# Twelve of sixteen activation differences formed on GpSimd, and a weight tile on the other side of SBUF: a diffusion layer on one Trainium2 core

## The chip, the cores and the metric

The kernel runs on one core of one Trainium2 chip. The metric is device time in microseconds (us) for one execution. TensorE (PE) multiplies matrices, VectorE (DVE), ScalarE (ACT) and GpSimd (POOL) work elementwise, and SyncE (SP) issues most of the DMA transfers. Each engine runs its own instructions strictly in order and waits for others by semaphores.

## The reference

One layer over 1024 latent tokens of width 1024, with 256 context tokens. What matters here is its second half, a gated MLP with a depthwise convolution of width 3 along the tokens:

```python
h2 = rms_norm(x, norm2_g[l]) * (1.0 + sc2) + sh2
x = x + g2 * conv_ffn(h2, w_up[l], conv_w[l], conv_b[l], w_down[l])

def conv_ffn(h, w_up, conv_w, conv_b, w_down):
    u = h @ w_up                      # 1024 x 1024 by 1024 x 5632
    up = jnp.pad(u, ((0, 0), (1, 1), (0, 0)))
    u = up[:, :-2] * conv_w[0] + up[:, 1:-1] * conv_w[1] + up[:, 2:] * conv_w[2] + conv_b
    a, b = jnp.split(u, 2, axis=-1)
    return (jax.nn.silu(a) * b) @ w_down
```

Everything is float32. The first half (a modulated RMSNorm, one input projection, retention and differential attention, one output projection) comes before it and is left as it is.

## The kernel before, in words

**Products in parts.** To keep float32's accuracy on TensorE, each operand is split into a high part `hi`, rounded to the matmul format by ScalarE (`nc.scalar.copy`), and a rest `lo`, formed on VectorE as `src - hi`. A product is three passes: hi·hi, hi·lo, lo·hi (`passes`, lines 130 to 132). Splitting a weight tile is `split_op` (lines 908 and 909); splitting an activation chunk is `split_to` (955 and 956).

**Seven products instead of eight.** The up projection multiplies 2x2 blocks by a Strassen-Winograd scheme. The activations are a 2x2 block matrix B11, B12, B21, B22 (channel halves by token halves), each of four chunks of 128 channels by 512 tokens. Besides B11, B21 and B22 themselves the products need four combinations, T1 = B12 - B11, T2 = B22 - T1, T3 = B22 - B12 and T4 = B21 - T2. `turned1` forms them, after the output projection: for each chunk `c`, TensorE transposes the normalised tokens (`turned`, line 948), ScalarE brings them out of PSUM with scale and shift (line 950) into `r12` and later `r22`, and the inner helper `less` (line 1015) forms the differences in place: per chunk `r12 - b11` (T1), `r22 - r12` (T3), `r22 - b11` (T2) and `b21 - b11` (T4). That makes sixteen differences of 128x512 float32, all on VectorE, and as many splits. `turned1` is a generator: `beside(turned1(), 0.36, 0.0)` advances it by 0.36 steps after each group of three matmuls of the first products, so TensorE meets the transposes at fixed places among them.

**The weight blocks.** Block `j` of 22 takes two weight tiles, `wra` (columns of the a half) and `wrb` (of the b half), 512 KB each. `up_load(j)` allocates and loads both; their pool `wst` has two buffers of each name on the right side of SBUF. From the two tiles GpSimd forms the weight sums (`combined`, lines 1054 and 1057 to 1060): for blocks from `NSUM` = 2 on these are s1 = b1 + b2 (1057), s2 = s1 - a1 (1058), s3 = a1 - b1 (1059) and a last one in place (1060); s2 feeds the product with T2, s3 the one with T3. For blocks 0 and 1 the sums were made earlier, during the output projection. The third block (`j == NSUM`) has a place of its own for its `wrb`, in the pool `third_b`, since both `wrb` buffers are still in use then. That pool is on the right side, where raw0, the rows x1 and r12, r22 lay before it: its load waits until these have been read. Its `wra` goes to a `wst` buffer that block 0 held, so its load waits until block 0's last use of it, the split for the product with T2.

**A block's products.** `chain` is one PSUM bank that accumulates through a block: after the product with T2 ScalarE copies it to `ua` (line 1144), after the one with T3 to `ub` (1152), after the one with T4 to `ub`'s other half (1160). The next product may only go on in the bank once the copy is done. VectorE adds the other products (1147, 1153, 1159), then follows the convolution (1095 to 1097), the gate's sigmoid-weighted unit (1165) and the product of the two halves (1166).

**What sets the order.** The list of each engine's instructions is written out by a scheduler when the kernel is built; pools and the written order decide it together. On the chip nothing is reordered.

Of the kernel before, what the change touches and what calls it, by code (L numbers as in the profile page):

```python
# [12 lines left out]
ALU = mybir.AluOpType  # L13
# [15 lines left out]
NF = DFF // P  # L29
# [44 lines left out]
def kernel(  # L74
# [16 lines left out]
    nc = tc.nc  # L91
# [61 lines left out]
    with ExitStack() as p1:  # L153
# [221 lines left out]
        side = {"g": iter(()), "rate": 0.0, "due": 0.0}  # L375
# [353 lines left out]
        class Unit:  # L729
# [34 lines left out]
            def turned(self, g):  # L764
                if self.aT is None:
                    self.aT = at.tile([P, NKT, P], F32, name="aT")
                n = min(4, NKT - 4 * g)
                nc.scalar.copy(self.aT[:, 4 * g : 4 * g + n, :], self.pt[g][:, :n, :])
# [101 lines left out]
    with ExitStack() as p2:  # L870
# [5 lines left out]
        for n in range(n_units + 8):  # L876
# [6 lines left out]
            if n in (8, 10, 12, 14):  # L883
                a, i = divmod(n // 2 - 4, 2)
# [27 lines left out]
    def raw_load(name, src, pool=None):  # L912
        o = (pool or wst).tile([P, KD, P], F32, name=name)
        nc.sync.dma_start(out=o, in_=src)
        return o
# [38 lines left out]
    def split_to(src, tt, c):  # L954
        nc.scalar.copy(tt[0][:, c, :], src)
        nc.vector.tensor_tensor(out=tt[1][:, c, :], in0=src, in1=r32(tt[0][:, c, :]), op=ALU.subtract)
# [7 lines left out]
    NPRE = 3  # L964
    NSUM = 2
    def up_load(j):
        return raw_load("wra", w_up[j]), raw_load("wrb", w_up[j + NF], third_b if j == NSUM else None)

    def sums_in_place(a, b):

# [40 lines left out]
    tmpT = tmpS.enter_context(tc.tile_pool(name="tmpT", bufs=1, side="right"))  # L1011

    def turned1():
        def less(o, a, b):
            nc.vector.tensor_tensor(out=o, in0=a, in1=b, op=ALU.subtract)

        for c in range(4):
            r12 = tmpT.tile([P, 512], F32, name="r12", bufs=2)
            turned(1, c, r12, True)
            b11 = raw0[:, c, :]  # L1020
            less(b11, r12, b11)
            yield
            r22 = tmpT.tile([P, 512], F32, name="r22")
            turned(1, c + 4, r22, True)
            split_to(b11, T1, c)
            split_to(r22, B22, c)
            less(r12, r22, r12)
            less(b11, r22, b11)
            split_to(r12, T3, c)
            yield  # L1030
        for c in range(4):
            b11, b21 = raw0[:, c, :], raw0[:, c + 4, :]
            split_to(b11, T2, c)
            less(b21, b21, b11)
            split_to(b21, T4, c)
            yield
# [27 lines left out]
    ops = [combined(j) for j in range(NSUM)]  # L1064
    split_ahead = []
    beside(turned1(), 0.36, 0.0)
    for j in range(NPRE):
        chain[j] = bank("chain", psA)
# [20 lines left out]
    with ExitStack() as p4:  # L1089
# [7 lines left out]
            nc.vector.scalar_tensor_tensor(out=t[:, : L - 1], in0=u[:, 1:], scalar=w[2], in1=t[:, : L - 1], op0=ALU.mult, op1=ALU.add)  # L1097
            return t

        third_b = p4.enter_context(tc.tile_pool(name="third_b", bufs=1, side="right", reuse_waits="tile"))  # L1100
        raws.append(up_load(NSUM))
        held = {}

# [66 lines left out]
        for j in range(NF):  # L1170
            if NSUM < j + 1 < NF:
                raws.append(up_load(j + 1))
            blk = Block(j)
            blk.begin()
            if last is not None:
                last.end()
                last.gated()
            blk.middle()
            last = blk
# [31 lines left out]
    with ExitStack() as p5:  # L1211
# [19 lines left out]
        def less(o, a, b):  # L1231
            nc.vector.tensor_tensor(out=o, in0=a, in1=b, op=ALU.subtract)
# [191 lines left out]
```

## Time and profile before

| | |
|---|---|
| time, median of 3 runs | 1449.69 us (1447.68 to 1451.36) |
| span of the profiled execution | 1444.3 us |
| around the span, against the median | 5.4 us |
| PE busy in the span | 1391.0 us (96%) |
| DVE busy | 1013.2 us (70%) |
| ACT busy | 738.7 us (51%) |
| POOL busy | 336.4 us (23%) |
| stage of the change | about 797 us (first chunk) to 880 us (fourth block) |

The profiled execution's own time is not listed apart from its span; the median of the three runs is 5.4 us longer than the span, and this is taken as what lies around it (start and end of the execution). The timeline's rows read: start in us, duration in us, engine, line, operation, output<-inputs, tile form; in square brackets the idle time of the engine before the row and what ended it. Rows of a line that start closer together than their duration are pipelined.

### The profile page before, as it was taken

To read this page: it belongs to the slowest core of one execution; us is meant where nothing else is said; L and a number is where in the kernel's file an instruction comes from. 1 tells how busy PE (TensorE), PEld (TensorE's weight loads), DVE (VectorE), ACT (ScalarE), POOL (GpSimd) and SP (SyncE) were. 2 spreads that over 40 slices of the span, in tenths; PEclk is the share of its full clock that TensorE was granted. 3 is DMA by queue.
4 is the path that set the end of the run, shared out by engine and by line. 5 is a ranking of instruction groups with operands and counts; after the bars stand their busy time and mean duration, and the time that the engine had idled before them with its cause. 6 is when DMAs were issued, how large, how long until landed. Compare 5 with 4: busy or idle time off the path is not lost.

```text
span 1444.3 us, 19462 instructions
## 1 busy us (share of the span) xinstructions
PE 1391.0 (96%) x6924; PEld 1143.5 (79%) x6924; DVE 1013.2 (70%) x1509; ACT 738.7 (51%) x1409; POOL 336.4 (23%) x450
## 2 busy tenths in 40 slices
PE   7999999999899989999999999999999999999996
PEld 2587888788778779999888877888888888888885
DVE  4687454443677588889455988788777777998457
ACT  4565212232355688998414654555555545455533
POOL 0220000022688422431121043222223320000001
PEclk9999999999999999999999999999999999999999
DMA  7548754466456676680422122222222224952224
GB/s 283 218 144 292 241 190 161 161 190 189 129 160 194 161 180 157 149 150 2 187 77 85 73 89 110 110 109 99 86 90 106 109 109 166 391 208 103 102 95 175
DMA packets 107529, 217.77 MB, mean 151 GB/s; under 512 B 8932, under 2 KB 47332, under 8 KB 106536
## 3 DMA queue, kind: packets, MB, share of 16 engines
q1 hardware_dynamic: 99304, 191.62, 38.2%
q0 software_dynamic: 8128, 24.91, 7.8%
q8 instruction: 55, 0.90, 0.3%
q14 instruction: 42, 0.34, 0.1%
HBM read 159.08 MB, written 57.41 MB: 150 GB/s over the span
## 4 chain that ended last, share of the span: by engine, by line
PE 69%; DVE 8%; issue 6%; DMA 6%; POOL 3%; ACT 3%; SPq 0%; POOLq 0%; DVEq 0%; ACTq 0%
PE pv L774 5%; PE pA L742 5%; PE chain L130 5%; PE chain L132 5%; PE chain L131 5%; PE c L132 4%; PE c L131 4%; PE c L130 4%; PE pn L132 3%; PE pn L130 3%; PE pn L131 3%; PE third L132 2%; PE third L130 2%; PE third L131 2%; PE pt L762 2%
## 5 line engine op out<-in xcount | busy, mean ns | idle before, releaser
L130 PE MATMUL chain<-T,whi 128*128 128x512 f32 x264 | 103.7, 393 | 5.8 <-ACT ub L1152 3.1
L130 PE MATMUL pl<-hT,whi 128*128 128x512 f32 x256 | 107.6, 422 | 0.7 <-ACT hT L583 0.7
L131 PE MATMUL chain<-T,whi 128*128 128x512 f32 x264 | 103.5, 392 | 0.0
L132 PE MATMUL chain<-T,wlo 128*128 128x512 f32 x264 | 103.1, 391 | 0.0
L131 PE MATMUL pl<-hT,whi 128*128 128x512 f32 x256 | 101.6, 397 | 1.6 <-DVE sm L115 1.3
L132 PE MATMUL pl<-hT,wlo 128*128 128x512 f32 x256 | 100.9, 394 | 0.0
L745 DVE TENSOR_REDUCE mt<-pA 128x1 f32<-128x1280 f32 x64 | 95.3, 1490 | 3.3 <-PE pA L742 1.2
L742 PE MATMUL pA<-ks,qhl 128*128 128x512 f32 (+1 forms) x384 | 91.4, 374 | 5.0 <-ACT p L749 5.0
L132 PE MATMUL c<-whi,ghl 128*128 128x512 f32 x232 | 90.4, 390 | 0.2 <-DVE ghl L1228 0.2
L130 PE MATMUL c<-whi,ghl 128*128 128x512 f32 x232 | 90.3, 389 | 0.0
L131 PE MATMUL c<-wlo,ghl 128*128 128x512 f32 x232 | 90.2, 389 | 0.0
L749 ACT ACTIVATE p<-pA,mt 128x1280 f32<-128x1280 f32 x64 | 85.5, 1336 | 4.6 <-DVE mt L745 4.5
L116 POOL TENSOR_TENSOR sm<-sm,mhalf 128x1 f32<-128x1 f32 x26 | 16.7, 641 | 294.9 <-DVE sm L115 294.8
L1057 POOL TENSOR_TENSOR cmb<-wrb 128x512 f32<-128x512 f32 x20 | 26.8, 1341 | 250.1 <-DMA wrb<-w_up 135.9
L908 ACT CAST whi<-cmb 128x512 fp32r<-128x512 f32 x62 | 38.6, 623 | 87.1 <-PE chain L131 65.3
L742 PEld LDWEIGHTS pA<-ks,qhl 128*128 128x128 f32 x384 | 68.8, 192 | 17.6 <-ACT p L749 6.1
L130 PE MATMUL pn<-whi,hT 128*128 128x512 f32 x192 | 77.8, 405 | 0.0
L774 PE MATMUL pv<-va,aT 128*128 128x128 f32 x640 | 77.0, 275 | 0.1
L399 ACT ACTIVATE st<-pn 128x512 f32<-128x512 f32 x30 | 17.9, 598 | 114.7 <-PE pn L132 97.2
L908 ACT CAST whi<-wra 128x512 fp32r<-128x512 f32 x55 | 33.7, 622 | 82.9 <-PE third L131 42.3
L132 PE MATMUL pn<-whi,hT 128*128 128x512 f32 x192 | 75.5, 393 | 0.0
L131 PE MATMUL pn<-wlo,hT 128*128 128x512 f32 x192 | 75.1, 391 | 0.0
(320 smaller groups left out, 4006.2 us busy)
## 6 DMA issues: line engine op xcount, KB each, us to landing
wm<-w_mod SPq DMA_DIRECT2D x32, 512.0 KB, 4.4
raw<-w_in SPq DMA_DIRECT2D x28, 512.0 KB, 4.5
wra<-w_up SPq DMA_DIRECT2D x24, 512.0 KB, 3.2
wrb<-w_up SPq DMA_DIRECT2D x23, 512.0 KB, 3.5
W<-w_down SPq DMA_DIRECT2D x44, 256.0 KB, 6.0
ad<-s SPq DMA_DIRECT2D x20, 512.0 KB, 3.7
wra<-ad SPq DMA_DIRECT2D x20, 512.0 KB, 3.2
wrb<-ad SPq DMA_DIRECT2D x18, 512.0 KB, 4.1
```

What stands on the lines that cost most here:

```text
L116: nc.gpsimd.tensor_tensor(out=out_ap, in0=out_ap, in1=mhalf[:, :n], op=ALU.pow)
L130: mm(ps, lh, rh, start=first, stop=False, skip_group_check=more)
L131: mm(ps, lh, rl, start=False, stop=False, skip_group_check=more)
L132: mm(ps, ll, rh, start=False, stop=last, skip_group_check=more)
L399: nc.scalar.activation(st.rearrange("p h e -> p (h e)"), pt, func, scale=scale)
L742: mm(self.pa[m][:, c0:c1], self.q[:, i, m, qs], self.k[:, m, c0:c1], start=(i == 0), stop=(i == 1))
L745: nc.vector.tensor_reduce(out=self.mt[:, m : m + 1], in_=self.pa[m][:, :LK], axis=AX.X, op=ALU.min)
L749: nc.scalar.activation(self.p[m], self.pa[m][:, :LK], AF.Exp, scale=-1.0, bias=self.mt[:, m : m + 1], accum_out=self.s[:, m : m + 1])
L762: nc.tensor.transpose(self.pt[g][:, i, :], self.p[0][:, (4 * g + i) * P : (4 * g + i + 1) * P], ident)
L774: mm(self.pv, self.aT[:, c, :], self.v[:, c, :], start=(c == 0), stop=(c == NKT - 1))
L908: nc.scalar.copy(hi, src)
L1057: nc.gpsimd.tensor_tensor(out=s1, in0=b1, in1=b2, op=ALU.add)
```

## The change

Two things are changed. In `turned1` the helper `less` takes an engine; the first difference of each chunk (T1) stays on VectorE, and the three others of each chunk, twelve of the sixteen, go to GpSimd. The pool `third_b` moves from the right side of SBUF to the left (where it follows the buffers of the combinations, on ground that the output projection's weights held), and for the third block `up_load` issues the load of `wrb` ahead of that of `wra`.

```diff
     def up_load(j):
-        return raw_load("wra", w_up[j]), raw_load("wrb", w_up[j + NF], third_b if j == NSUM else None)
+        if j == NSUM:
+            b = raw_load("wrb", w_up[j + NF], third_b)
+            return raw_load("wra", w_up[j]), b
+        return raw_load("wra", w_up[j]), raw_load("wrb", w_up[j + NF])
...
     def turned1():
-        def less(o, a, b):
-            nc.vector.tensor_tensor(out=o, in0=a, in1=b, op=ALU.subtract)
+        def less(o, a, b, eng=nc.gpsimd):
+            eng.tensor_tensor(out=o, in0=a, in1=b, op=ALU.subtract)
 
         for c in range(4):
             r12 = tmpT.tile([P, 512], F32, name="r12", bufs=2)
             turned(1, c, r12, True)
             b11 = raw0[:, c, :]
-            less(b11, r12, b11)
+            less(b11, r12, b11, nc.vector)
             yield
...
-        third_b = p4.enter_context(tc.tile_pool(name="third_b", bufs=1, side="right", reuse_waits="tile"))
+        third_b = p4.enter_context(tc.tile_pool(name="third_b", bufs=1, reuse_waits="tile"))
```

The lines behind the edit stand three lower in the changed kernel (`less` is 1018 there, s1 1060, s2 1061, the copy to `ua` 1147). The first place is VectorE's list, from the first difference to the split of block 0's weights for T2 (`wlo_8013`); here are its first eleven rows before (r12_7740 and r22_7758 belong to the first chunk, r12_7794 to the second; yT11 is the low part of T1 or B22).

```order
L1015 TENSOR_TENSOR raw0_7039<-r12_7740,raw0_7039 128x512
L1015 TENSOR_TENSOR r12_7740<-r22_7758,r12_7740 128x512
L956 TENSOR_TENSOR yT11_4752<-r22_7758,yT01_4750 128x512
L956 TENSOR_TENSOR yT11_4752<-raw0_7039,yT01_4750 128x512
L956 TENSOR_TENSOR T31_7720<-r12_7740,T30_7719 128x512
L1015 TENSOR_TENSOR raw0_7039<-r22_7758,raw0_7039 128x512
L1015 TENSOR_TENSOR raw0_7039<-r12_7794,raw0_7039 128x512
L909 TENSOR_TENSOR wlo_7848<-wra_7422,whi_7847 128x512
L1015 TENSOR_TENSOR r12_7794<-r22_7811,r12_7794 128x512
L956 TENSOR_TENSOR yT11_4752<-raw0_7039,yT01_4750 128x512
L956 TENSOR_TENSOR yT11_4752<-r22_7811,yT01_4750 128x512
```

The same place on VectorE in the changed kernel:

```order
L1018 TENSOR_TENSOR raw0_7039<-r12_7740,raw0_7039 128x512
L956 TENSOR_TENSOR yT11_4752<-r22_7758,yT01_4750 128x512
L956 TENSOR_TENSOR yT11_4752<-raw0_7039,yT01_4750 128x512
L956 TENSOR_TENSOR T31_7720<-r12_7740,T30_7719 128x512
L1018 TENSOR_TENSOR raw0_7039<-r12_7794,raw0_7039 128x512
L909 TENSOR_TENSOR wlo_7848<-wra_7422,whi_7847 128x512
L956 TENSOR_TENSOR yT11_4752<-raw0_7039,yT01_4750 128x512
L956 TENSOR_TENSOR yT11_4752<-r22_7811,yT01_4750 128x512
```

From the first L1015 to `wlo_8013` the list has 39 rows before and 28 now: the twelve differences are gone, and one split of T4 that stood behind `wlo_8013` stands ahead of it. All these rows but one (an addition out of PSUM) read both inputs from SBUF. The second place is GpSimd's list behind the last sum of block 1 (`cmb_7728`), in the changed kernel; wrb_8007 and wra_8009 are the third block's tiles.

```order
L1057 TENSOR_TENSOR cmb_7728<-wrb_7428,wra_7426 128x512 [waits PE_49,Activation_49]
L1018 TENSOR_TENSOR r12_7740<-r22_7758,r12_7740 128x512 [waits DMAHW4_49,DMAHW5_49,DMAHW3_49,DMAHW6_49,DVE_49,Activation_49]
L1018 TENSOR_TENSOR raw0_7039<-r22_7758,raw0_7039 128x512 [waits DVE_49]
L1018 TENSOR_TENSOR raw0_7039<-raw0_7039 128x512 [waits Pool_49]
...
L1018 TENSOR_TENSOR r12_7886<-r22_7904,r12_7886 128x512 [waits DVE_49,Activation_49]
L1018 TENSOR_TENSOR raw0_7039<-r22_7904,raw0_7039 128x512 [waits DVE_49]
L1018 TENSOR_TENSOR raw0_7039<-raw0_7039 128x512 [waits Pool_49]
L1060 TENSOR_TENSOR cmb_8120<-wrb_8007 128x512 [waits DMAHW3_49]
L1061 TENSOR_TENSOR cmb_8121<-cmb_8120,wra_8009 128x512 [waits DMAHW4_49,DVE_49,Pool_49]
```

Before, the third block's s1 followed `cmb_7728` directly; now the twelve differences stand between them. The third place is ScalarE's list around block 0's copy to `ua` (chain_7730 is block 0's bank, cmb_8121 the third block's s2), before:

```order
L908 CAST whi_8131<-wrb_7428 128x512 [waits PE_49]
L1144 COPY ua_7787<-chain_7730 128x512 [waits PE_49]
L1095 ACTIVATE tconv_8067<-ua_7787,cl_63 128x1024 [waits DVE_49,Activation_49]
L908 CAST whi_8167<-cmb_8121 128x512 [waits Pool_49]
L1152 COPY ub_8011<-chain_7730 128x512 [waits PE_49]
```

and in the changed kernel:

```order
L908 CAST whi_8131<-wrb_7428 128x512 [waits PE_49]
L908 CAST whi_8167<-cmb_8121 128x512 [waits PE_49,Pool_49]
L1147 COPY ua_7787<-chain_7730 128x512 [waits PE_49]
L1098 ACTIVATE tconv_8067<-ua_7787,cl_63 128x1024 [waits DVE_49]
L908 CAST whi_8185<-cmb_8120 128x512 [waits PE_49,Activation_49]
L1155 COPY ub_8011<-chain_7730 128x512 [waits PE_49]
```

The rounding of the third block's s2, which waits for GpSimd, stood behind the copy to `ua` and ahead of the copy to `ub`; now it stands ahead of both. SyncE's list still has the two loads as its next weight loads, with wrb first, and the load of wra still waits for VectorE's `wlo_8013`.

## The prediction

> **What bounds the kernel now.** I read the page first, then the windows around the change, the waits of TensorE, and the timeline of each engine there.
>
> ```profile
> span 1444.3 us, 19462 instructions
> PE 1391.0 (96%) x6924; PEld 1143.5 (79%) x6924; DVE 1013.2 (70%) x1509; ACT 738.7 (51%) x1409; POOL 336.4 (23%) x450
> ```
>
> TensorE is busy 96% of the span, so only its gaps can be won, and whatever makes a new gap is lost. By stages (columns: stretch, its length, then busy time of PE, PEld, DVE, ACT, POOL):
>
> ```profile
> 799.08:822.83 23.75, 23.75 (x117) 19.55 (x117) 23.64 (x41) 20.15 (x36) 0.00 (x0) 1.00 0.00 1
> 1000.00:1100.00 100.00, 100.00 (x443) 82.81 (x442) 80.45 (x92) 52.86 (x76) 27.49 (x20) 1.00 0.30 110
> ```
>
> The first stretch is the one of the differences: TensorE never idle, VectorE as full (23.64 of 23.75), GpSimd empty. The second is the steady run of later blocks: TensorE has no gap at all, a matmul each 100/443 = 0.226 us. A delay that reaches the steady run is not caught up there. TensorE's waits at the first blocks:
>
> ```profile
> PE chain L130 <- ACT ub L1152: 3.1, 1, 3.1
> PE chain L130 <- ACT ua L1144: 2.7, 2, 2.1
> ```
>
> Where the 3.1 comes from, in order of time:
>
> ```profile
> 799.08 0.69 DVE L1015 TENSOR_TENSOR raw<-r,raw 128x512 f32<-128x512 f32 x1
> 822.15 0.68 DVE L909 TENSOR_TENSOR wlo<-wra,whi 128x512 fp32r<-128x512 f32 x1
> 822.99 0.33 SPq L914 DMA_DIRECT2D wra<-w_up  x1
> 823.50 0.33 SPq L914 DMA_DIRECT2D wrb<-w_up  x1
> 825.55 0.59 ACT L1144 COPY ua<-chain 128x512 f32<-128x512 f32 x1 [2.35 <-PE chain L132]
> 828.71 1.29 POOL L1057 TENSOR_TENSOR cmb<-wrb 128x512 f32<-128x512 f32 x1 [32.35 <-DMA wrb<-w_up]
> 830.08 2.12 POOL L1058 TENSOR_TENSOR cmb<-cmb,wra 128x512 f32<-128x512 f32 x1
> 832.24 0.62 ACT L908 CAST whi<-cmb 128x512 fp32r<-128x512 f32 x1 [3.12 <-POOL cmb L1058]
> 832.76 0.58 ACT L1152 COPY ub<-chain 128x512 f32<-128x512 f32 x1
> 833.39 0.67 PE L130 MATMUL chain<-T,whi 128*128 128x512 f32 x1 [3.05 <-ACT ub L1152]
> ```
>
> VectorE ends its list with the split of block 0's weights at 822.83, only then is the third block's `wra` buffer free, its loads go out at 822.99 and 823.50, GpSimd's s2 ends at 832.20, and ScalarE, which stands at the rounding of s2, does the copy to `ub` late. So VectorE's list sets the date of the loads, and the loads that of the copy.
>
> **VectorE's list.** The change takes twelve rows out of it, each about 0.69 us long:
>
> ```profile
> L1015 DVE TENSOR_TENSOR raw<-r,raw x8: 681/682/686, 799.1 to 814.3; 128x512 f32<-128x512 f32 x8
> L1015 DVE TENSOR_TENSOR r<-r,r x4: 683/684/692, 799.9 to 812.5; 128x512 f32<-128x512 f32 x4
> ```
>
> They overlap a little: 39 rows in 23.75 us are 0.61 a row. The 28 rows that are left would take 17.1 us. But GpSimd now works beside them, on the same kind of operands, and this the trace has priced at the fourth block:
>
> ```profile
> 860.57 1.53 POOL L1057 TENSOR_TENSOR cmb<-wrb 128x512 f32<-128x512 f32 x1 [6.12 <-DVE wlo L909]
> 861.47 1.18 DVE L909 TENSOR_TENSOR wlo<-cmb,whi 128x512 fp32r<-128x512 f32 x1
> 862.17 1.62 POOL L1058 TENSOR_TENSOR cmb<-cmb,wra 128x512 f32<-128x512 f32 x1
> 862.57 1.77 DVE L909 TENSOR_TENSOR wlo<-wra,whi 128x512 fp32r<-128x512 f32 x1
> 863.75 1.74 POOL L1059 TENSOR_TENSOR cmb<-wra,wrb 128x512 f32<-128x512 f32 x1
> 864.87 1.17 DVE L909 TENSOR_TENSOR wlo<-wra,whi 128x512 fp32r<-128x512 f32 x1
> 865.57 1.63 POOL L1060 TENSOR_TENSOR wrb<-wra,cmb 128x512 f32<-128x512 f32 x1
> ```
>
> Read the ends: POOL 862.10, DVE 862.65, POOL 863.79, DVE 864.34, POOL 865.49, DVE 866.04, POOL 867.20. They take turns, one GpSimd and one VectorE row each 1.70 us (862.10, 863.79, 865.49, 867.20), and nothing runs at once. A GpSimd row therefore costs VectorE 1.70 - 0.61 = 1.09 us while VectorE always has work. Twelve cost 13.1. The list ends at 799.08 + 17.1 + 13.1 = 829.3, not at 822.83: **6.5 us later**, though it is twelve rows shorter. Bounds for the price of a GpSimd row: 0, as where VectorE idles or reads PSUM, and 1.29, its whole length alone (the row at 828.71). I take 1.09, since the rows are of the same size, type and engines. The price at which the list ends as before is (23.75 - 17.1)/12 = 0.55.
>
> [...]
>
> ```profile
> 822.61 0.39 PE L130 MATMUL chain<-T,whi 128*128 128x512 f32 x1
> ```
>
> TensorE meets the same delay earlier. Between its need of T1's last chunk and block 0's product with T2 (822.61) stand 39 matmuls, 8.8 us, so it asks at 813.8. The chunk's split is the 20th VectorE row, with some seven GpSimd rows ahead: 799.08 + 20 x 0.61 + 7 x 1.09 = 819, a wait of five us, and the product with T2 at about 828. This isn't added: the list's end is later. ScalarE's eviction of `r22` now waits for GpSimd too, with the casts of T1 to T4 queued behind it; that is in the turns.
>
> **The third block's loads.** `wrb` no longer waits for raw0's ground and is in long before; its part costs nothing, and s1 is done while `wra` is awaited. But `wra` still waits for the split at the list's end: 829.3 + 0.16 (822.83 to 822.99) = 829.5.
>
> ```profile
> DMA to landing us min/median/max: 3.1/3.2/11.2
> ```
>
> That is the `wra` tile's loads; I take 3.2, as it now travels ahead of the rest (5.2, from 823.50 to 828.71, is the other end, where the pair shared the queue). Landed at 832.7, s2 until 834.0 (1.29), its rounding until 834.6 (0.62). And here the new order bites: the copy to `ua` stands behind this rounding, so it starts at 834.6 instead of 825.55, 9.0 later.
>
> **From the copy to the steady run.** Before, 13.8 us lay between the copy at 825.55 and the matmul at 839.36, since the copy to `ub` was late. That wait falls away. What is left is a chain of rows:
>
> ```profile
> 829.15 1.93 DVE L1096 SCALAR_TENSOR_TENSOR tconv<-ua,cl,tconv 128x1023 f32<-128x1023 f32 x1 [1.37 <-ACT tconv L1095]
> 840.68 1.28 DVE L1096 SCALAR_TENSOR_TENSOR tconv<-ub,cl,tconv 128x1023 f32<-128x1023 f32 x1
> 835.95 1.28 ACT L1165 ACT_TABLE_LOAD   x1 [2.08 <-DVE tconv L1097]
> 837.24 1.06 ACT L1165 ACTIVATE tconv<-tconv 128x1024 f32<-128x1024 f32 x1
> 838.73 0.59 ACT L1144 COPY ua<-chain 128x512 f32<-128x512 f32 x1
> 839.36 0.50 PE L130 MATMUL chain<-T,whi 128*128 128x512 f32 x1 [0.67 <-ACT ua L1144]
> ```
>
> Copy to L1096: 829.15 - 825.55 = 3.6; L1096 itself 1.9, as s3 runs beside it again; the addition to `ub` 0.6; L1097 1.3; table load 1.3; activation to the matmul 839.36 - 837.24 = 2.1. Sum 10.8. TensorE stands at block 1's product with T3 at 834.6 + 10.8 = 845.4 instead of 839.36: **6.0 us later**. Between, it has 31 matmuls (7.0 us) from about 835.3, so it is done at 842.3 and waits 3.1. What such a wait costs more shows here (two rows behind the 3.05 us wait, and two at the 2.07 us one):
>
> ```profile
> 833.86 0.63 PE L131 MATMUL chain<-T,whi 128*128 128x512 f32 x1
> 834.28 0.63 PE L132 MATMUL chain<-T,wlo 128*128 128x512 f32 x1
> 871.70 0.50 PE L130 MATMUL chain<-T,whi 128*128 128x512 f32 x1 [2.07 <-ACT ua L1144]
> 872.03 0.40 PE L131 MATMUL chain<-T,whi 128*128 128x512 f32 x1
> ```
>
> After 3.05 us matmuls last 0.63, after 2.07 they are at 0.40 at once. Before paid this stretch too, ahead of 839.36; in the changed kernel it would fall behind it. A slow matmul takes 834.28 - 833.86 = 0.42 from start to start and not 0.226, so a stretch of eight costs 1.6. I count it, since 3.1 is on the side of 3.05; the other end is 0. The 2.07 us wait at 871.70 I leave as it is (its end would be -2.1).
>
> **Sum.** +6.0 + 1.6 = +7.6 us: the profiled execution would go from 1444.3 to 1451.9, and with the 5.4 us around it from the median of 1449.69 to **1457.3**. A measurement of this kernel tells about 0.3% (4.4 us) from no change.
>
> **Rivals.** *The rows run side by side (0.14).* Then VectorE's list isn't the limit. The last eviction of `r22`:
>
> ```profile
> 811.51 0.78 ACT L950 ACTIVATE r<-pt,m 128x512 f32<-128x512 f32 x1
> ```
>
> GpSimd's last three differences follow it with 1.37 each (828.71 to 830.08), until 816.4, casts and splits until 818, `wra` is in at 822, and the copy to `ua` runs at its old 825.55. With 10.8 from there TensorE is at 836.4, 3.0 earlier: 1446.7, and 1444.6 where the 2.07 us wait goes too. It decides below 0.55 us per GpSimd row. For it: GpSimd is empty there and the twelve rows fit its time; against it: the seven rows above.
>
> *The delay is mostly given back (0.14).* The turns come as reckoned, but the 3.1 us wait stays under what slows the clock, and the 2.07 us wait is gone, as the third block's weights then lead: 6.0 - 2.1 = +3.9, 1453.6. For it: 2.07 us cost no clock. Against it: the 2.07 wait came from VectorE's own rows, which stay.
>
> *It runs away (0.12).* Full 1.29 per row (+2.4), a load of 5.2 (+2.0): +12.0, 1461.7. [...]
>
> *The change doesn't do what it says* in one half in any case: `wrb` goes first, but `wra` and s2, which ScalarE waits for, come no sooner.
>
> **How the numbers follow.** Forecast 0.60, 1454 to 1461. The range leaves out most of the first rival and the far end of the third: 1449.5 to 1462. Faster by over 0.3%: half of the first rival, 0.07. Within 0.3%: its other half and most of the second, 0.20. Slower: the rest, 0.73.
>
> **What would show it.** Right: GpSimd's twelve rows at 1.6 to 1.7 us instead of 1.3, VectorE's rows beside them at 1.2 to 1.8, taking turns; `wlo` of block 0 ending near 829; the load of `wra` behind it; TensorE waiting some five us for T1's last chunk and again for the copies to `ua`. Wrong: GpSimd's rows at 1.3 with VectorE's at 0.69 beside them, the copy to `ua` still at 825 to 826, or the first product of the fifth block, before at
>
> ```profile
> 874.55 0.39 PE L130 MATMUL chain<-yT,whi 128*128 128x512 f32 x1
> ```
>
> not later by 4 us or more.

## The result and the profile after

The changed kernel takes 1458.53 us (median of 4 runs, 1456.91 to 1460.3) beside 1450.34 us for the kernel before (4 runs, 1447.68 to 1451.36). The ratio of the medians is 1.0056; the ratio estimated from all runs is 1.0066, with a 95% interval of 1.0047 to 1.0086: slower, by 0.5 to 0.9%. The forecast was 1457.3 us. The page of the profiled execution after:

```profile
span 1455.7 us, 19463 instructions
PE 1398.5 (96%) x6924; PEld 1147.9 (79%) x6924; DVE 1018.9 (70%) x1497; ACT 740.3 (51%) x1409; POOL 352.6 (24%) x462
```

Twelve instructions have gone from VectorE (1509 to 1497), yet its busy time has grown from 1013.2 to 1018.9 us. That is the result in one line: what was taken away came back as waiting that the profile counts as work (VectorE's rows of 0.68 us take up to 1.78 beside GpSimd's). This run's time was 1457.44, so 1.7 us lie around the span, not the 5.4 that the front matter inferred from a span of one run and a median of others.

In this execution the stage begins 1.38 us later than before (first difference at 800.46, not 799.08), from small waits hundreds of microseconds ahead of the change. Differences below are given with these 1.38 us taken off. The stage by windows (stretch, length, then busy time of PE, PEld, DVE, ACT, POOL, each with its rows), from the first difference to the end of block 0's split, and in the steady run:

```profile
800.46:830.16 29.70, 23.81 (x101) 18.38 (x101) 29.12 (x30) 19.67 (x34) 19.27 (x12) 0.89 0.05 18
1000.00:1100.00 100.00, 100.00 (x443) 82.81 (x442) 78.22 (x90) 50.96 (x74) 29.26 (x22) 1.00 0.31 111
```

The stretch was 23.75 us and is 29.70. VectorE is still full in it (29.12), and TensorE, which never paused there before, is busy for 23.81 of it. The steady run is the same as before: nothing is given back. Grouped by line and shape, GpSimd's differences and three of VectorE's groups in the stage (busy us, then mean ns of one):

```profile
L1018 POOL TENSOR_TENSOR raw<-r,raw 128x512 f32<-128x512 f32 x4 | 6.7, 1680 | 2.5 <-DVE yT L956 2.5
L1018 POOL TENSOR_TENSOR raw<-raw 128x512 f32<-128x512 f32 x4 | 6.4, 1611 | 0.3
L1018 POOL TENSOR_TENSOR r<-r,r 128x512 f32<-128x512 f32 x4 | 6.2, 1547 | 6.8 <-ACT r L950 6.1 <-DVE raw L1018 0.7
L956 DVE TENSOR_TENSOR T<-r,T 128x512 fp32r<-128x512 f32 x4 | 6.0, 1490 | 0.0
L1018 DVE TENSOR_TENSOR raw<-r,raw 128x512 f32<-128x512 f32 x4 | 4.9, 1228 | 0.0
L1047 DVE TENSOR_TENSOR ua<-second,ua 128x512 f32<-128x512 f32 x1 | 0.7, 678 | 0.0
```

VectorE rows that took 0.68 us before now average 1.2 to 1.5 in the groups shown (one that waits for its turn is counted as busy); the one that reads an input from PSUM (`ua<-second`) keeps its 0.68, beside GpSimd's row of 813.57. TensorE's waits in the stage and the blocks after it, and the rows that answer to those of the chain before, in order of time:

```profile
PE fifth L130 <- ACT yT L955: 4.5, 1, 4.5
PE chain L130 <- ACT ua L1147: 4.1, 2, 2.1
...
```

```profile
820.99 0.55 PE L130 MATMUL fifth<-yT,whi 128*128 128x512 f32 x1 [4.47 <-ACT yT L955]
827.21 0.33 SPq L914 DMA_DIRECT2D wrb<-w_up  x1
827.42 0.63 PE L131 MATMUL fifth<-yT,whi 128*128 128x512 f32 x1
829.48 0.68 DVE L909 TENSOR_TENSOR wlo<-wra,whi 128x512 fp32r<-128x512 f32 x1
830.18 0.33 SPq L914 DMA_DIRECT2D wra<-w_up  x1
833.43 1.39 POOL L1061 TENSOR_TENSOR cmb<-cmb,wra 128x512 f32<-128x512 f32 x1 [1.52 <-DMA wra<-w_up]
833.70 0.39 PE L130 MATMUL chain<-T,whi 128*128 128x512 f32 x1
836.45 0.62 ACT L908 CAST whi<-cmb 128x512 fp32r<-128x512 f32 x1 [2.15 <-PE chain L131]
836.97 0.58 ACT L1147 COPY ua<-chain 128x512 f32<-128x512 f32 x1
847.59 0.50 PE L130 MATMUL chain<-T,whi 128*128 128x512 f32 x1 [2.05 <-ACT ua L1147]
885.78 0.56 PE L130 MATMUL chain<-yT,whi 128*128 128x512 f32 x1
```

TensorE waits 4.47 us for T1's last chunk and then runs at 0.63 us a matmul for a while (the granted clock is 0.53 from 820.99 to 828.21, and 1.00 from there to 833.70, with matmuls of 0.40), so its product with T2 begins at 833.70 and not 822.61. VectorE's list ends late, and the load of `wra` goes out behind it. The copy to `ua` stands at 836.97 and not 825.55, the product with T3 at 847.59 and not 839.36, the fifth block at 885.78 and not 874.55. From there to the end of the span it is 569.9 us, before 569.75.

### The profile page after: what moved, and what is told of

Its sections match the earlier page's. It is cut to its first block, busy times and chain, and to the rows that moved or that the text cites. A ratio compares the mean times of both kernels' runs of the same rounds, so it can differ in the third digit from the quotient of the medians.

```text
span 1455.7 us, 19463 instructions
## 1 busy us (share of the span) xinstructions
PE 1398.5 (96%) x6924; PEld 1147.9 (79%) x6924; DVE 1018.9 (70%) x1497; ACT 740.3 (51%) x1409; POOL 352.6 (24%) x462
## 4 chain that ended last, share of the span: by engine, by line
PE 71%; DVE 9%; DMA 5%; issue 3%; ACT 3%; POOL 3%; SPq 0%; POOLq 0%; DVEq 0%; ACTq 0%
PE chain L130 5%; PE chain L131 5%; PE chain L132 5%; PE pv L774 5%; PE pA L742 5%; PE c L132 4%; PE c L131 4%; PE c L130 4%; PE pn L131 3%; PE pn L132 3%; PE pn L130 3%; PE third L132 2%; PE third L131 2%; PE third L130 2%; PE pt L762 2%
```

## The experiments

The theory that was tested: GpSimd's rows and VectorE's rows with both inputs in SBUF don't run at once but in turns. Rival A: the cost is GpSimd's own slowness, and the splits that wait for it. Rival B: the cost is the other half of the change, the place and order of the third block's weights. To keep noise ahead of the stage out, the table gives for each kernel's profiled execution the stretch from the first difference to the end of the last split of T4, and the time from that first difference to the end of the span; the ratio is the one estimated from all runs.

| kernel | stretch, us | from there on, us | ratio to before (95%) |
|---|---|---|---|
| before | 24.36 | 645.2 | |
| after | 29.09 | 655.2 | 1.0066 (1.0047 to 1.0086) |
| differences only | 29.08 | 654.3 | 1.0055 (1.0035 to 1.0075) |
| weights' side only | 24.37 | 646.0 | 0.9998 (0.9985 to 1.0011) |
| idle rows that read | 33.90 | 657.3 | 1.0062 (1.0040 to 1.0084) |
| idle rows that write | 24.36 | 648.5 | 1.0018 (1.0005 to 1.0032) |
| T4's four only | 25.93 | 649.1 | 1.0043 (1.0030 to 1.0056) |
| after, early half | 29.08 | 653.7 | 1.0056 (1.0040 to 1.0072) |
| before, early half | 24.37 | 649.7 | 1.0045 (1.0029 to 1.0060) |
| idle rows, one column | 24.36 | 644.7 | 1.0024 (1.0008 to 1.0039) |

The middle column is one execution of each kernel. Two executions of one kernel (before, early half) agree in it to 0.1 us, but the first difference starts anywhere from 797.5 to 803.5 us in these profiles, so the medians differ from this column by up to 5 us.

**The differences only.** The edit of `turned1` on the kernel before, and nothing else:

```diff
-        def less(o, a, b):
-            nc.vector.tensor_tensor(out=o, in0=a, in1=b, op=ALU.subtract)
+        def less(o, a, b, eng=nc.gpsimd):
+            eng.tensor_tensor(out=o, in0=a, in1=b, op=ALU.subtract)
...
-            less(b11, r12, b11)
+            less(b11, r12, b11, nc.vector)
```

> The kernel before with only the twelve differences on GpSimd; the third block's second weight tile stays on its old side and is loaded after the first one. Theory (each GpSimd difference beside a full VectorE makes the pair take turns: VectorE's own row of 0.68 us becomes about 1.75, so twelve moved rows save 12 x 0.68 = 8.2 us and cost about 12 x 1.08 = 13 us): VectorE's list of the stage ends 5 to 7 us later than before, the kernel is 6 to 10 us slower, so all of the change's cost is here. Rival A (GpSimd's own slowness: a difference takes 1.6 us instead of 0.68 and the splits wait for it): the same time, but VectorE's other rows stay at 0.68 us and VectorE shows idle time instead, some 6 us of it. Rival B (the place and the order of the third block's weights make the change slow): within 2 us of before.

Measured: 1456.21 us beside 1447.31, and a stretch of 29.08 us, the changed kernel's to 0.01. The rows beside each other have the same durations as after, VectorE's idle time in the stretch is 0.6 us, not 6. So the cost sits in this half, which puts rival B out, and not in VectorE waiting for results, which puts rival A out.

**The weights' side only.** The kernel after with `eng=nc.vector` as the default of `less`.

> The kernel after with the twelve differences put back on VectorE; only the third block's second tile is on the other side and loaded first. Theory: VectorE's rows of the stage all take 0.68 us, its list ends where it did before (within 0.5 us), and the time is that of before, within 0.3% (1446 to 1452 us); at best 1.5 us less if the second tile lands earlier. Rival A says the same. Rival B: 1456 us or more.

Measured: 1448.1 us beside 1447.31, no difference. Here a row showed that nobody had expected. The third block's s1 starts at 822.59, beside a full VectorE:

```profile
822.59 8.74 POOL L1060 TENSOR_TENSOR cmb<-wrb 128x512 f32<-128x512 f32 x1 [22.50 <-DMA wrb<-w_up]
829.49 0.69 DVE L909 TENSOR_TENSOR wlo<-wrb,whi 128x512 fp32r<-128x512 f32 x1
830.09 0.69 DVE L1150 TENSOR_TENSOR ua<-fifth,ua 128x512 f32<-128x512 f32 x1
```

It lasts 8.74 us instead of 1.29, while VectorE's rows keep their 0.69: it did not get a turn until VectorE came to a row that reads PSUM (830.09; 831.33 less 1.29 is 830.04). In these rows the two engines excluded each other, but not by turns. What decides that became the second question.

**Idle rows that read, idle rows that write.** The kernel before, and behind the last difference of each chunk three GpSimd rows that nobody needs; in the second kernel they only write, behind a difference of one column that holds them in their place:

```diff
+        idle = tmpT.tile([P, 512], BF16, name="idle")
...
+            for _ in range(3):
+                nc.gpsimd.tensor_tensor(out=idle, in0=b11, in1=b11, op=ALU.subtract)
```

```diff
+            nc.gpsimd.tensor_tensor(out=idle[:, :1], in0=b11[:, :1], in1=b11[:, :1], op=ALU.subtract)
+            for _ in range(3):
+                nc.gpsimd.memset(idle, 0.0)
```

> The kernel before, with all differences on VectorE, and twelve more GpSimd rows of 128x512 that read a chunk of the turned activations (both inputs, a finished one), three behind each chunk, and write a spare bf16 tile that nobody reads. No instruction waits for them but the three sums of the third block behind them on GpSimd, and the load of that block's second tile. Theory: nothing is saved, and twelve pairs take turns at about 1.7 us each, so VectorE rows beside them show 1.7 us, VectorE's list of the stage ends 12 x 1.08 = 13 us later than before, and the kernel is 9 to 15 us slower. Rival A (GpSimd's rows hurt only those who wait for their results): VectorE's rows stay at 0.68 us, within 2 us of before. Rival B: also within 2 us of before.

> As the run with twelve idle GpSimd rows, but each of the twelve rows only writes the spare tile (a memset of 128x512 bf16), behind one difference of 128x1 for each chunk that puts them at the same place in the list. Theory: it is the reading of SBUF that takes turns, so VectorE's rows stay near 0.68 us and the time is that of before within 2 us. If the writes take turns too, VectorE shows rows of 1 us and more beside the memsets and the time is 3 us or more above before; then the theory's word 'reading' is too narrow.

Measured: the reading rows cost 9.9 us (1457.22 beside 1447.31) though no VectorE row waits for them; this too speaks against rival A. The third group of them, and the rows beside them:

```profile
815.40 4.25 POOL L1031 TENSOR_TENSOR idle<-raw 128x512 bf16<-128x512 f32 x3 [2.50 <-DVE raw L1015]
815.78 1.52 DVE L956 TENSOR_TENSOR T<-r,T 128x512 fp32r<-128x512 f32 x1
817.22 1.52 DVE L1015 TENSOR_TENSOR r<-r,r 128x512 f32<-128x512 f32 x1
818.67 1.52 DVE L956 TENSOR_TENSOR yT<-raw,yT 128x512 fp32r<-128x512 f32 x1
820.12 0.68 DVE L956 TENSOR_TENSOR yT<-r,yT 128x512 fp32r<-128x512 f32 x1
```

Three turns, then 0.68 again. A turn is 1.45 us here and not 1.70 (these rows have one source tile and a bf16 result; which of the two shortens the turn was not tried), so a row costs VectorE 0.85 (1.45 less its pitch of 0.60); eleven full turns, and 0.24 for the one that began beside a PSUM row, give 9.6, and the stretch is 9.54 longer. The expectation took 1.08 and was 3.5 too high. The writes cost the stretch nothing: twelve memsets of 0.53 us, no VectorE row of the stage longer than before. So twelve rows that read lengthened the stretch by 9.54 us, and twelve that only write by none. What the second one loses (2.5 us) comes of its rows of one column. One of them was shut out:

```profile
813.71 14.97 POOL L1030 TENSOR_TENSOR idle<-raw 128x1 bf16<-128x1 f32 x1 [1.35 <-DVE raw L1015]
```

It reads raw0 until 828.7, and the load of the third block's `wrb`, on that ground, is issued 29.5 us behind the first difference instead of 24.4; TensorE then waits 5.5 us for the copy to `ub`, before 3.1.

**T4's four only.** `less(b21, b21, b11, nc.gpsimd)` on the kernel before, the other twelve on VectorE.

> The kernel before with only the four differences of T4 on GpSimd, the last ones of the stage. Theory (a price for each pair of turns): the stretch from the first difference to the last split of T4, 24.36 us before and 29.08 with twelve, is 24.36 + 4/12 x 4.72 = 25.9 us; no early wait of TensorE (T1 and T3 are formed as before), so the time is 1 to 3 us above before. Rival (the cost is that of the chain through the two row buffers of T3's difference, which make TensorE wait 4.5 us for T1): nothing of it is left with T4 alone, the stretch is within 0.5 us of 24.36 and the time within 1 us of before.

Measured: a stretch of 25.93, as forecast to 0.03, but by other means, and 1452.77 us beside 1446.85, 5.9 more and not 1 to 3.

```profile
803.96 1.68 POOL L1015 TENSOR_TENSOR raw<-raw 128x512 f32<-128x512 f32 x1 [6.68 <-DVE raw L1015]
808.67 1.68 POOL L1015 TENSOR_TENSOR raw<-raw 128x512 f32<-128x512 f32 x1 [3.04 <-DVE raw L1015]
814.59 9.55 POOL L1015 TENSOR_TENSOR raw<-raw 128x512 f32<-128x512 f32 x2 [4.24 <-DVE raw L1015]
816.32 0.74 PE L130 MATMUL fifth<-yT,whi 128*128 128x512 f32 x2 [1.60 <-ACT yT L955]
823.58 2.34 DVE L956 TENSOR_TENSOR T<-raw,T 128x512 fp32r<-128x512 f32 x3 [1.85 <-ACT T L955]
```

Two differences took their turn, the third was shut out until VectorE ran out of work at 821.7, and then VectorE waited 1.85 us for T4. So here the shut-out difference lengthened the stretch by coming late, and a price for each pair does not tell it all. That this wait cost the kernel time is not shown: the expectation "no early wait of TensorE" failed. T1's last chunk was late all the same. TensorE waited 1.60 us for it and ran slow behind it (rows of 0.63 us from 819.02 to 820.30, ahead of the wait 0.39), so that its product with T2 began 27.46 us behind the first difference, before 23.53. Those 3.9 us are all that this execution loses from the first difference on.

**After, early half.** The prediction let the load of `wra` and s2 set the copy to `ua`; the rounding ahead of that copy shows a wait for TensorE. To tell them apart, the half of `wra` that s2 and s3 read gets a tile of its own:

```diff
+    def halves(src):
+        a1 = third_b.tile([P, 4, P], F32, name="a1")
+        nc.sync.dma_start(out=a1, in_=src[:, 0:4, :])
+        a2 = wst.tile([P, KD, P], F32, name="wra")
+        nc.sync.dma_start(out=a2[:, 4:8, :], in_=src[:, 4:8, :])
+        return a1, a2[:, 4:8, :]
...
-            return raw_load("wra", w_up[j]), b
+            return halves(w_up[j]), b
...
```

> The kernel after, with the half of the third block's first weight tile that its sums two and three read in a tile of its own, which does not wait for the last split of the first block's weights. The prediction held that this load (issued at the end of VectorE's list, landed 3.2 us later) sets the first copy of the stage's results; the trace of after says that TensorE's product with T2 came last there. If TensorE is it: the copy to the first block's upper half stands where it did (within 0.7 us of 36.5 us behind the stage's first difference), and the time is within 2 us of after (1456.5 to 1460.5 beside a before of 1450.3, or ratio 1.0045 to 1.008). If the load is it: the copy comes 2 to 3 us earlier and the time is 2 to 4 us less.

Measured: the load leaves 2.5 us earlier against the stage's start, the rounding still waits for TensorE, and the copy comes 35.59 us behind the first difference, after 36.51, before 26.47. The ratio is 1.0056, that of after within both intervals.

```profile
833.05 0.39 PE L130 MATMUL chain<-T,whi 128*128 128x512 f32 x1
835.80 0.62 ACT L908 CAST whi<-cmb 128x512 fp32r<-128x512 f32 x1 [2.15 <-PE chain L131]
836.32 0.58 ACT L1155 COPY ua<-chain 128x512 f32<-128x512 f32 x1
```

TensorE came last, here as in the kernel after. The copy's 0.9 us are not the load's: the product with T2 itself began 32.32 us behind the first difference, after 33.24, since the slow matmuls behind the wait for T1 ended sooner (10 rows of 0.62 us and more, after 13). That is more than the 0.7 us that the expectation allowed for, but the trace shows no gain to the copy from the earlier load.

The same holds for the other kernels with differences on GpSimd. Counted from the first difference, the product with T2 began later than before by 9.7 us (after), 9.0 (differences only), 8.8 (this one) and 3.9 (T4's four), and the time from the first difference on is longer by 10.0, 9.1, 8.5 and 3.9. So in these four the cost equals, within 0.4 us, what TensorE loses ahead of its product with T2: the waits for T1 and the slow matmuls behind them. That is the balance and not every step: behind the copy the kernel after wins 3.2 us back, as the wait of 3.1 us is gone, and loses 3.0 again in two more slow stretches. With the idle rows that read it doesn't hold (8.9 and 12.1).

**Before, early half.** The same tile in the kernel before, with `third_b` opened ahead of the pool `up`, on ground that is free after the last transposes. It was meant to beat both kernels, by ending the wait of 3.1 us.

> The kernel before, all differences on VectorE, with the same half in a tile of its own, and both that tile and the second weight tile on ground that is free as soon as TensorE has done its last transposes (they are laid out ahead of the pool of the convolution's tiles). In the kernel before, the sum two of the third block runs at 830.08 to 832.20, ScalarE's rounding of it waits 3.12 us and TensorE 3.1 us for the copy behind that rounding. Theory: the loads are issued 6 to 8 us earlier, sum one runs beside the full VectorE (one pair of turns, 0.4 to 1.1 us on VectorE's list, or none if it is shut out as in the run with the weights' side alone), sum two when VectorE has split the first combination (about 827), so the rounding comes some 3 us earlier, the wait of 3.1 us falls to under 1, and the time is 2 to 4 us below before. Rival (turns): the sums push VectorE's list back by 3 us and more, and the time is that of before or up to 3 us above.

Measured: 1454.05 us beside 1446.85, slower; a second profile shows the same rows. s1 was shut out until VectorE's list had ended (824.9):

```profile
812.89 13.15 POOL L1068 TENSOR_TENSOR cmb<-wrb 128x512 f32<-128x512 f32 x1 [18.06 <-DMA wrb<-w_up]
827.41 0.62 ACT L908 CAST whi<-cmb 128x512 fp32r<-128x512 f32 x1 [5.76 <-POOL cmb L1069]
827.93 0.58 ACT L1155 COPY ua<-chain 128x512 f32<-128x512 f32 x1
```

The rounding of s2 is 3.3 us earlier against the stage's start, as expected, but the scheduler put it ahead of the copy to `ua`, as in the kernel after, and the copy is 3.9 later: TensorE waits 7.8 us for two copies, before 5.8 in three waits. The theory missed the order of ScalarE's list, which is fixed when the kernel is built.

> The kernel before with the early half once more, for a second profile: the first was of its fastest run (1449.09 us; the median was 1454.05), and showed the third block's sum one shut out for 13.15 us and TensorE waiting 7.8 us for two copies behind ScalarE's rounding of sum two. If the slow runs come from turns, sum one takes 1.3 to 1.8 us here and VectorE shows a row of 1.8; if shutting out is the rule, the same 13 us row shows at a time of 1452 us or more, and the difference to 1449 lies in the granted clock.

Both profiles have the row of 13.15 us and 649.7 and 649.8 us from the first difference on; the 6 us between them lie ahead of the stage.

**Turn or shut out?** Four kernels were for this. The first is the one with idle rows, one column wide:

> The run with twelve idle GpSimd rows that read, but each row reads and writes one column (128x1) instead of 512. In the run with memsets two of four such narrow rows lasted 1.72 and 14.97 us beside a full VectorE whose rows stayed at 0.68 us, and the wide rows took turns. If the width decides: these rows are shut out until VectorE pauses or reads PSUM, several of them show 2 us and more, VectorE's rows stay at 0.68 to 0.75 us and the stretch of the stage within 0.5 us of 24.36. If the row's width only sets the price of a turn: the rows take 0.3 to 0.8 us each, VectorE's rows beside them about 0.2 us more, and the stretch is 1 to 3 us longer. The time is within 3 us of before in both.

Measured: neither. All twelve rows came in at the next row of VectorE (1.72 us for three), and VectorE's rows stayed at 0.68. The times scatter from 1444.14 to 1454.54 us and the profile is of the fastest execution, so what makes the ratio 1.0024 is not shown. The other three compute nothing of the reference: runs of VectorE rows, with a GpSimd difference released by one of them. In short, for independent rows (`zt_before` is the result of the trial before, which ties each trial to it):

```python
for r in range(16):
    nc.vector.tensor_tensor(out=outs[r % 4], in0=zt_before if r == 0 else s0, in1=xt if r == 3 else s1, op=sub)
    if r == 3:
        nc.gpsimd.memset(xt[:, :fill], 0.0)
        nc.gpsimd.tensor_tensor(out=zt, in0=xt, in1=s1, op=sub)
```

> A kernel that computes nothing of the reference: 36 trials, in each VectorE runs 16 rows of 128x512 with two inputs in SBUF, and a GpSimd difference is released by the fourth row, after a memset of 16 to 456 columns that shifts its start against VectorE's rows in steps. Trials 1 to 12: the GpSimd row is 128x512 and VectorE's rows do not depend on each other; 13 to 24: each VectorE row reads what the one before wrote; 25 to 36: as the first twelve with a GpSimd row of one column. In the traces so far some GpSimd rows came in at VectorE's next row boundary (VectorE row 1.5 to 1.8 us) and some were shut out until VectorE stopped (8.7 to 15 us). If the moment of the start against VectorE's rows decides: within a group of twelve the trials divide by the memset's length, one stretch of lengths turned and another shut out. If the dependence of VectorE's rows decides: the first and second group differ as a whole. If the width decides: the third group differs as a whole. If it is chance: no order in it. Where every trial takes turns, shutting out needs something that this kernel lacks.

Measured: neither the start's phase nor the width decided here. With independent rows the trials alternated strictly, turn, shut out, turn, at 512 columns (1.27 to 1.81 us against 7.73 to 8.06) and at one (0.20 to 0.74 against 6.66 to 6.99); with rows that each read the one before, all twelve took turns (1.26 to 1.60 us; each of those VectorE rows starts 0.03 us behind the end of the one before it). GpSimd's timeline:

```profile
7.00 1.47 POOL L116 TENSOR_TENSOR z<-x,s 128x512 f32<-128x512 f32 x1
17.74 8.06 POOL L116 TENSOR_TENSOR z<-x,s 128x512 f32<-128x512 f32 x1
28.65 1.40 POOL L116 TENSOR_TENSOR z<-x,s 128x512 f32<-128x512 f32 x1
```

> Five groups of ten trials of the kind of the last run (16 VectorE rows each, one GpSimd difference of 128x512 released by the fourth row; nothing of the reference is computed). There the trials with independent VectorE rows took turns and were shut out one after the other, whatever the start's phase, and those whose rows each read the row before all took turns. Two things alternated there: the tile that GpSimd reads, and whether VectorE had paused since GpSimd's row before (it pauses behind a shut-out row, not behind one that took its turn). Group 1 changes the tile every second trial only: if the tile decides, the trials go turn, turn, shut, shut; if the pause decides, turn, shut, turn, shut. Group 2 makes VectorE pause behind each trial: if the pause decides, all take turns. Group 3: each VectorE row reads the row before the last; if it is the reading of the row just ahead that lets GpSimd in, this group behaves as independent rows. Group 4: two GpSimd rows in a trial: if the pause decides, the second of a pair is shut out. Group 5 repeats the chained rows: all turns.

Measured: with the tile changed every second trial still turn, shut, turn, shut (1.38 and 7.94 us; VectorE pauses 1.15 us behind a shut-out one); with a pause behind each trial ten turns of ten (1.32 to 1.38); rows that read the row before the last gave turn and shut in alternation, as independent ones (1.38 and 8.00); chained rows took turns (1.50). So in these trials the pause decided, not the tile; the chained rows, with a pause of 0.03 us at each, fit that. Two differences in a trial both took turns (3.04 us for the pair) or both were late (9.34): that part was expected otherwise, and fits if a turn itself counts as a break.

> Trials of 22 independent VectorE rows, each trial behind a pause of VectorE (nothing of the reference is computed). Group 1, 14 trials: the GpSimd difference of 128x512 is released by the row k behind the pause, k from 1 to 14. Group 2, 12 trials: a first difference is released by row 2 and takes its turn, a second one by row 2+k, k from 2 to 13. Group 3: as group 2, with a GpSimd memset of 512 columns behind the first difference. So far every difference that asked up to 6 VectorE rows behind a pause or a turn took its turn, with one exception behind a memset, and those that asked 7 rows and more behind one were shut out. Theory (a stretch of some 7 unbroken VectorE rows, 4.2 us, shuts GpSimd out): group 1 turns up to k of about 6 and is shut out above; group 2 alike, counted from the first turn. Rival (each stretch of VectorE's rows gives GpSimd one turn, whenever it asks, and is then closed): group 1 takes turns at every k, the second difference of group 2 is shut out at every k. If the memset matters, group 3 differs from group 2.

Measured: a clear edge, and the rival is out. Behind a turn the edge is near the 4.2 us of the theory, behind a pause it comes sooner than the expected six rows. Here VectorE's first row and GpSimd's difference in the fourth and the fifth trial of the first group, and the first and second difference in the trials k = 7 and k = 8 of the second:

```profile
51.61 0.69 DVE L111 TENSOR_TENSOR o<-z,s 128x512 f32<-128x512 f32 x1 [1.44 <-POOL z L116]
54.85 1.58 POOL L113 TENSOR_TENSOR x<-s,s 128x512 f32<-128x512 f32 x1 [3.28 <-DVE o L111]
67.45 0.69 DVE L111 TENSOR_TENSOR o<-z,s 128x512 f32<-128x512 f32 x1 [1.44 <-POOL z L116]
71.30 10.61 POOL L113 TENSOR_TENSOR x<-s,s 128x512 f32<-128x512 f32 x1 [3.88 <-DVE o L111]
311.08 1.57 POOL L113 TENSOR_TENSOR x<-s,s 128x512 f32<-128x512 f32 x1 [2.08 <-DVE o L111]
316.36 1.58 POOL L113 TENSOR_TENSOR x<-s,s 128x512 f32<-128x512 f32 x1 [3.70 <-DVE o L111]
327.98 1.58 POOL L113 TENSOR_TENSOR x<-s,s 128x512 f32<-128x512 f32 x1 [2.07 <-DVE o L111]
333.86 7.60 POOL L113 TENSOR_TENSOR x<-s,s 128x512 f32<-128x512 f32 x1 [4.30 <-DVE o L111]
```

Behind a pause of VectorE, a request after 3.24 us (51.61 to 54.85) took its turn, one after 3.85 (67.45 to 71.30) and all later ones were shut out until VectorE stopped (10.61 down to 5.19 us). Behind a turn, 3.71 (312.65 to 316.36) still turned, 4.30 (329.56 to 333.86) did not. With a memset in between it was the same: 3.70 turned (1.57 us), 4.31 did not (7.60). The layer's kernels fit: in the kernel with T4's four, 3.03 us behind the last turn came in and 4.24 was shut out, though VectorE had ended a row out of PSUM 2.5 us before; after's longest gaps, 2.56 and (s1) 3.97, came in; the 8.74 and 13.15 us rows asked more than ten microseconds behind VectorE's last pause. One thing stays open: the idle rows of one column didn't delay VectorE (its rows kept 0.68 to 0.69), and three of them came in at 810.16, 11.7 us behind VectorE's last pause, where the wide rows' edge would have shut them out.

## Why the prediction was right

- **The turns.** Forecast: VectorE's list ends 6.5 us later, at 1.09 us for each GpSimd row. Measured: 23.75 to 29.70, 5.95 later. 28 rows at 0.61 and 0.59 of idle time leave 12.0 us for twelve rows, 1.0 each: the first (801.28) began while VectorE waited, one (813.57) ran beside a PSUM row. The idle rows, whose results nobody needs, show that it is the sharing. Right, and for the reason given; that all twelve took turns was luck of the list, since GpSimd never let more than 2.56 us pass between them. One reading behind the price is wrong, "nothing runs at once": at the fourth block VectorE's rows of 860.87 (0.67 us) and 864.26 (0.68), which read PSUM and are not among the seven shown, ran beside GpSimd's. The turns that end at 863.79 and 867.20 have no such row in them, so the 1.70 us stand.
- **The full price.** 1.29, a GpSimd row's whole length alone, was the upper bound and the third rival's +2.4. No run shows a row that cost VectorE that much: the rows say 1.0 on average, 1.09 for a full turn. Which engine waited differed: after's VectorE rows took up to 1.78 us in turns, and a shut-out GpSimd row 13.15.
- **The loads.** `wra` was forecast to leave at 829.5 and to land 3.2 later; it left at 830.18 (828.80 with the 1.38 off), and s2 began 3.25 later. Wrong: "`wrb` no longer waits for raw0's ground and is in long before". It left at 827.21, as the split of T3's last chunk ended, which reads r12 (in the kernel with the weights' side only it left right behind that split too). So its new ground is, by all appearance, in part that of r12, and the account of that ground ahead of the prediction is incomplete; addresses were not read. It cost nothing, as s2 had to await `wra` anyway.
- **The copy to `ua`.** Forecast 9.0 later, measured 10.0. The size was nearly right, the reason was not: the step "This isn't added: the list's end is later" failed. TensorE's own delay was put at a product with T2 "at about 828"; it began at 833.70 (832.3 with the 1.38 off), as the wait for T1 ended at 820.99 and slow matmuls (0.63) filled the next 7 us. Of the 9.7 us, 4.47 are the wait for T1, put at five; 1.4 are two short waits (0.77 for an eviction by ScalarE, 0.61 for T1's low part); most of the rest are the slow matmuls, which the sum put at nothing. TensorE, not s2, came last, and the early half in the kernel after showed it. That the two paths end within 2 us of each other, so that the wrong one gave nearly the right size, was luck.
- **From the copy to the product with T3.** Forecast 10.8, measured 10.62. The product stands 6.85 later, not 6.0.
- **The slow matmuls.** One stretch of 1.6 us was counted, for a wait of 3.1. The wait was 2.05, was followed by matmuls of 0.63 us all the same (granted clock 0.63 from 847.59 to 851.50), and so was the next one of 2.08 at the fourth block (0.63 from 881.70 to 885.80), whose stretch was not in the sum. Each stretch cost about the 1.6 reckoned (eight matmuls at 0.43 us from start to start, not 0.23). This is the mis-sized term, two stretches and not one: the fifth block stands 9.85 later, not 7.6.

```profile
848.16 0.39 PE L132 MATMUL chain<-T,wlo 128*128 128x512 f32 x1
848.63 0.63 PE L131 MATMUL chain<-T,whi 128*128 128x512 f32 x1
882.31 0.40 PE L130 MATMUL chain<-T,whi 128*128 128x512 f32 x1
882.80 0.63 PE L132 MATMUL chain<-T,wlo 128*128 128x512 f32 x1
```

- **The rivals.** Side by side: excluded, no VectorE row with both inputs in SBUF ran so. Given back: no, neither the slow stretch nor the wait at the fourth block went away, and the rest is 569.9 beside 569.75 us. Run away: neither its price of 1.29 (1.0 on average) nor its load of 5.2 (s2 began 3.25 behind the issue) came. The total fell inside the forecast's own range, with the profiled execution at +9.85 and the medians 8.2 apart.

## What to carry to other kernels

Moving an elementwise row of 128x512 with two SBUF inputs from a full VectorE to GpSimd saved 0.61 us here and cost 1.0 to 1.09 where it took its turn: a full VectorE got fuller. Where it was shut out VectorE's rows kept their 0.68, but its result came some 7 us late (8.30 us for a row of 1.29, with T4's four). GpSimd's rows of 128x512 were free here only while VectorE idled (1.26 us at 832.17 before, within 2.29 of idle time) or read PSUM (0.68 beside the row of 813.57 after), or where they only wrote (twelve memsets of 0.53); count those moments before moving a row. And follow the waits of the engine that is 96% busy: here the kernel lost what TensorE lost at one early wait and behind it, not what the late load cost. Last, read the list of the engine that others wait for: whatever is rounded earlier may be put ahead of a copy that TensorE needs sooner.

## What the runs showed of the hardware, unexpected

- In the trials and stages shown here a GpSimd row of 128x512 with SBUF input that asked while VectorE ran unbroken rows with two SBUF inputs took a turn up to 3.24 us behind VectorE's last pause, or 3.97 behind its last giving way; from 3.85 and 4.24 us on it was shut out until VectorE paused or read PSUM (rows of 4.59 to 13.15 us), while VectorE's rows kept 0.68 to 0.69. The durations of these rows, 1.26 us alone (832.17 before), 1.53 to 1.75 in after's turns and up to 13.15 shut out, were thus no measure of their work.
- In the first blocks, waits of TensorE of 2.00 to 2.08 us were followed by matmuls of 0.63 us in seven cases (two each in after, differences only and after with the early half, one with the weights' side only), but not in two, where they stayed at 0.40: behind 2.07 us at 871.70 before, and behind 2.08 in the kernel with idle rows that write. A wait of 3.14 us in the kernel with the weights' side only was followed by 0.40 throughout:

```profile
842.51 0.50 PE L130 MATMUL chain<-T,whi 128*128 128x512 f32 x1 [3.14 <-ACT ua L1147]
842.85 0.40 PE L131 MATMUL chain<-T,whi 128*128 128x512 f32 x1
```

The length of the wait alone did not decide it here; what does was not tried.
